# The place of one gate unit, and a parameter tile 40 columns wider

## The chip, the cores and the metric

The kernel runs on one core of a Trainium2 chip. The metric is the time of one execution on the device in microseconds. Five engines work side by side: TensorE (PE; its weight loads are listed apart as PEld), VectorE (DVE), ScalarE (ACT), GpSimd (POOL) and SyncE (SP), which in this kernel issues the transfers (DMA). Every engine runs its own instructions in a fixed order and waits at semaphores for the others.

## What is computed

One layer of a flow-matching backbone over 1152 tokens: 1024 latent ones and 128 of context, each with 1024 channels. Cut to what matters here:

```
proj = h @ w_in                                  # 1024 -> z, xBC, dt, u, v, ga, gb
y_ssd = rmsnorm((scan(conv(xBC), dt) + D*x) * silu(z))
y_sgu = u * (sgu_w @ layernorm(v) + sgu_b)       # in chunks of 128 positions
merged = sigmoid(ga) * (y_ssd @ w_bs) + sigmoid(gb) * (y_sgu @ w_bu)
x = x + gate1 * rmsnorm(merged @ w_out)
up = conv3x3(h2 @ w_up)                          # 1024 -> 2 x 2816
x = x + gate2 * rmsnorm((gelu(up_a) * up_val) @ w_down)
```

All in float32. Each large product is computed with operands split into a high and a low part in a reduced format: high x high, high x low and low x high, so three matmuls per block.

## The kernel before

**Weights.** A class `Weights` (lines 58 to 104) works through one list of weight blocks, `plan`, in which each block is 128 x 512. `_load` brings a block into a raw tile `wr` (three buffers), `_split` makes from it the high part `wh` on ScalarE (L82) and the low part `wl` on VectorE (L83), four buffers each. `advance(n)` splits the next n blocks and keeps loads three ahead; `take(n)` hands out the next n pairs of parts. For some blocks a `room` is given, and their parts go there in place of `wh` and `wl`: six of the eight blocks of each half of v go into `vwh` and `vwl` (lines 891 to 894), and four of the last blocks of the down projection go into `wacc`, which reuses the `acc` tiles (lines 1299 to 1305).

**Units of the input projection.** `inproj` (L422) computes one block of 128 output channels for all tokens: three groups of 24 matmuls over 384 tokens each (`gemm_cm`, L299 to L301), each into a PSUM bank `gps`. Between the groups it splits weights ahead. A `sink` then takes the bank out. There are three such banks (`gbank`), and the v tiles use them too. For a gate unit (`gate_unit`, L615) the sink copies the bank on ScalarE into a tile `gt` (L618) and sends it by a DMA to DRAM (L619), where the merge stage will fetch it. The tile comes from the pool that `gtp.p` names.

**The scan and what comes after.** In the rounds of lines 847 to 869 the scan of 16 head pairs runs beside units of x, z and gates, which fill TensorE. `gtp.p` is then the scan's pool `ssdA`, with one `gt` buffer (L839). Twelve of the 16 gate units run there. The last round is the last z unit alone. L870 closes the scan's pools. The pools opened next lie over the same memory: `right` (with `gt`, now three buffers, L874), `yu` (where `vwh` and `vwl` lie) and `sgu` (with `vtok`). A tile laid over closed ones waits until these are no longer read or written.

Then comes v in two halves (lines 984 to 1004). For each half a gate unit runs first and then nine v tiles (`v_tile`, L901), one per 128 tokens: 24 matmuls with 512 moving columns into one bank, a copy into `vtok` on ScalarE (L910) and statistics on VectorE. Ahead of the first half, `v_ahead(8)` splits all eight blocks of v with a priority 400 places earlier than its place in the program (`P_V`). Two more gate units run behind the eight u units.

**The order.** The instructions of each engine are put in order at compile time: place in the program is the priority, `tc.high_priority(offset=n)` moves a block n places forward, and a model of the engines says when an instruction could start. On the chip, each engine keeps that order.

**The feed-forward part** (from L1164). A pool `ffn` holds the parameters `fpar` (nine taps and a bias for 44 channel blocks), four padded tiles `U`, the accumulators `acc` and the split activations `gh` and `gl`. For each of 22 steps `up_gemm` computes two channel blocks (`pup`), `ffn_conv` applies nine taps (one on ScalarE, eight on VectorE, L1200) and `pair_end` forms gelu times value. `down_mm` (L1207) computes the down projection: 128 tokens of `gh` or `gl` are the weights of a matmul, and 512 columns of `wh` or `wl` are the moving operand, into a bank `fo` (L1212 to L1214). The first third of the tokens is computed in the steps, 18 matmuls at a time, as its activations become ready; the other two thirds follow without a pause, with `gh` and `gl` built from DRAM.

**Places in memory.** The memory of each partition is given out as a stack. The pool `w` has eleven tiles of 2048 bytes (three `wr`, four `wh`, four `wl`). The pools `ssd...`, then `yu`, `sgu` and `br`, and at last `ffn` begin at its end. Inside a pool tiles stand one behind the other, each starting at a multiple of 32 bytes. In `ffn` the order is: `fpar`, four U tiles of 18 x 66 x 4 = 4752 bytes, then `acc`, `gh`, `gl` and the rest.

Of the kernel before, what the change touches and what calls it, by code (L numbers as in the profile page):

```python
# [4 lines left out]
F32 = mybir.dt.float32  # L5
# [25 lines left out]
MT_DT, MT_U, MT_B, MT_C, MT_X, MT_Z, MT_GA, MT_GB = 0, 1, 9, 13, 17, 33, 49, 57  # L31
# [75 lines left out]
def body(tc, A, O):  # L107
# [10 lines left out]
    def close(*cms):  # L118
        for cm in cms:
            cm.__exit__(None, None, None)  # L120
# [10 lines left out]
    ga_scr = dr.tile([8, 128, T], F32, name="ga_scr")  # L131
    gb_scr = dr.tile([8, 128, T], F32, name="gb_scr")
# [17 lines left out]
    gate_mts = [MT_GA + i for i in range(8)] + [MT_GB + i for i in range(8)]  # L150
# [46 lines left out]
    W = Weights(nc, wp, plan)  # L197
# [95 lines left out]
    def gemm_cm(ps, parts, kh, kl, cols, first=True, last=True):  # L293

        n = len(parts) * 4
        for k in range(n):
            wh, wl = (p.rearrange("p (k m) -> p k m", m=128)[:, k % 4, :] for p in parts[k // 4])
            xh, xl = kh[:, k, cols], kl[:, k, cols]
            PE.matmul(ps, lhsT=wh, rhs=xh, start=first and k == 0, stop=False)  # L299
            PE.matmul(ps, lhsT=wh, rhs=xl, start=False, stop=False)  # L300
            PE.matmul(ps, lhsT=wl, rhs=xh, start=False, stop=last and k == n - 1)  # L301
# [11 lines left out]
    def gbank(name):  # L313
        return pg.tile([128, 512], F32, tag="g", name=name)
# [71 lines left out]
    parts = {}  # L386
# [33 lines left out]

    def inproj(sink, parts=None):
        parts = parts or W.take(2)
        for tb in range(NTB):
            ps = gbank("gps")[:, :TB]
            gemm_cm(ps, parts, hh, hl, slice(TB * tb, TB * tb + TB))
            W.advance(1 if tb else 0)
            sink(tb, ps)
            yield  # L430

# [2 lines left out]
    def run_unit(u, step=None):  # L434
        gen, tails = u
        for _ in gen:
            if pending:
                pending.pop(0)()
            if step:
                step()  # L440
        while pending:
            pending.pop(0)()
        pending.extend(tails)
# [119 lines left out]
    def b_unit(g, inp=True):  # L563
        BT = spe.tile([128, GW], F32, tag="BT", name=f"BT{g}")
        Bt = spe.tile([128, NC, 128], F32, tag="Btok", name=f"Btok{g}")
        groups[g] = [BT, Bt]
        return conv_gen(BT, 16 + g, inp), [lambda b=b: to_tok(BT, Bt, f"B{g}", b) for b in range(3)]

    def c_unit(g):
        CT = spb.tile([128, GW], F32, tag="CT", name=f"CT{g}", bufs=2)  # L570

        def cb(b):
            if b == 0:
                groups[g] += [CT, spe.tile([128, 2, NC, 128], F32, tag="CB", name=f"CB{g}")]
            BT, _, _, CB = groups[g]
            pv = tbank(f"pcb{g}{b}")[:, :384].rearrange("p (c i) -> p c i", i=128)
            for i in range(3):
                o = gcol(384 * b + 128 * i)
                PE.matmul(pv[:, i, :], lhsT=BT[:, o:o + 128], rhs=CT[:, o:o + 128], start=True, stop=True)
            for d in range(2):  # L580
                V.tensor_tensor(CB[:, d, 3 * b:3 * b + 3, :], pv, (Lo, Up)[d].unsqueeze(1).to_broadcast([128, 3, 128]), op=ALU.mult)
        return conv_gen(CT, 20 + g), [lambda b=b: cb(b) for b in range(3)]

    def x_unit(q):
        X = spb.tile([128, GW], F32, tag="X", name=f"X{q}", bufs=3)

        def tok(b):
            if b == 0:
                xq[q] = (X, spa.p.tile([128, NC, 128], F32, tag="Xtok", name=f"Xtok{q}", bufs=2))
            to_tok(X, xq[q][1], f"X{q}", b)  # L590
        return conv_gen(X, q), [lambda b=b: tok(b) for b in range(3)]

    def z_unit(q):
        X = xq[q][0]

        def gen():
            zt = spr.tile([128, T], F32, tag="z", name=f"z{q}")

            def sink(tb, ps):
                S.activation(zt[:, TB * tb:TB * tb + TB], ps, AF.Copy, scale=0.5)  # L600
            yield from inproj(sink)
            silu(zt)
            for t0, t1, s in segs(0, T):
                xs = X[:, gcol(t0):gcol(t0) + t1 - t0]
                V.tensor_tensor(xs, xs, zt[:, t0:t1], op=ALU.mult)
                S.activation(zt[:, t0:t1], xs, AF.Square)
            V.tensor_tensor(ssq, ssq, zt, op=ALU.add)
            S.activation(X, X, AF.Copy, scale=par[:, P_SN + q:P_SN + q + 1])
            SP.dma_start(yssd_scr[q], X)
        return gen(), []  # L610
# [1 line left out]
    class gtp:  # L612
        pass

    def gate_unit(dst, parts=None):  # L615
        def sink(tb, ps):
            o = gtp.p.tile([128, TB], F32, tag="gt", name="gt", bufs=gtp.bufs)
            S.copy(o, ps)  # L618
            SP.dma_start(dst[:, TB * tb:TB * tb + TB], o)  # L619
        return inproj(sink, parts), []  # L620

    def unit_of(mt):
        if mt >= MT_GB:
            return gate_unit(gb_scr[mt - MT_GB])
        if mt >= MT_GA:
            return gate_unit(ga_scr[mt - MT_GA])
        if mt >= MT_Z:
            return z_unit(mt - MT_Z)
        if mt >= MT_X:
            return x_unit(mt - MT_X)  # L630
        if mt >= MT_C:
            return c_unit(mt - MT_C)
        return b_unit(mt - MT_B)
# [169 lines left out]
    def merge(fills, steps):  # L803

        nf = 3 * len(fills)
        st = {"k": 0, "d": 0}

        def adv():
            with tc.high_priority(offset=P_SCAN):
                steps[st["d"]]()  # L810
            st["d"] += 1

        def step():
            st["k"] += 1
            while st["d"] < len(steps) * st["k"] // nf:
                adv()
        for f in fills:
            run_unit(unit_of(f), step)
        while st["d"] < len(steps):
            adv()  # L820

    def flush():
        while pending:
            pending.pop(0)()
# [22 lines left out]
    for q in range(17):  # L847
        steps = []
        if q < 16:
            if after is None:  # L850
                flush()
                pro, outs = ssd(q)
                steps += pro + outs
            else:
                steps += after
            after = None
            if q + 1 < 16 and (q + 1) % 4:
                lazy = []

                def nxt_steps(i, q=q, lazy=lazy):  # L860
                    if not lazy:
                        flush()
                        lazy.extend(ssd(q + 1))
                    return lazy[0][i]()
                steps += [lambda i=i, f=nxt_steps: f(i) for i in range(4)]
                after = lazy
        merge(rounds[q], steps)
        if after is not None:
            after = after[1]
    close(sa_cm, sb_cm, se_cm, k_cm, sr_cm)  # L870


# [23 lines left out]
    def v_ahead(n):  # L896

        with tc.high_priority(offset=P_V):
            W.advance(n)
# [74 lines left out]
    def loads(c):  # L974
        if c == 0:
            queue_behind(SP.dma_start(cc.rearrange("p s k -> p (s k)"), A["cond"].to_broadcast([128, 2048])), W.last)
        elif c == 1:
            SP.dma_start(wsT, A["sgu_w"])
            SP.dma_start(sb, A["sgu_b"].to_broadcast([128, 1024]).rearrange("p (g i) -> p g i", g=8))
        elif c < 4:  # L980
            mod_load1()
            mod_load1()

    for h in range(2):
        gate = W.take(2)
        if h == 0:
            v_ahead(8)
        run_unit(gate_unit((gb_scr if gate_mts[h] >= MT_GB else ga_scr)[(gate_mts[h] - MT_GA) % 8], gate))
        if h:
            W.advance(6)  # L990
        parts = W.take(8)
        for c in range(NC):
            cpy = v_tile(h, c, parts)
            if h == 0 and c < 4:
                loads(c)
            if h == 0 and c == 3:
                queue_behind(S.activation(cc, cc, AF.Silu), cpy)
            if h or c >= 4:
                mod_step()
            if h == 0 and c in (6, 7):  # L1000
                bias(c - 6)
            if h and c % 3 == 2:
                layernorm(c // 3)
        W.advance(2)
# [66 lines left out]
    gate = gate_tile(0)  # L1071
# [90 lines left out]


    f_cm, fp = pool("ffn")  # L1164
    fpar = fp.tile([128, 440], F32, name="fpar")
    SP.dma_start(fpar, A["fpar"])

    U = [[fp.tile([128, 18, 66], F32, name=f"U{i}{j}") for j in range(2)] for i in range(2)]
# [66 lines left out]
    for kk in range(NFF):  # L1235
# [19 lines left out]
        else:  # L1255
            for half in range(1 if kk == 1 else 0, 2):
                parts = W.take(2)
# [138 lines left out]
```

## Time and profile before

| | us |
|---|---|
| median of 3 runs | 2447.7 (2444.2 to 2451.8) |
| the profiled execution | 2446.1 |
| its span, first to last instruction | 2444.3 |
| ScalarE busy | 1191.6 |
| DMA, share of 16 engines | 41.1% |

The profile shows one execution. A row of a timeline gives the start from the beginning of the span, the length, the engine, the line, the operation, the tiles written and read, and in brackets the idle time of the engine just before and what ended it. Matmuls overlap: one is shown some 0.33 to 0.40 us long while the next starts 0.17 to 0.23 us behind it, so their spacing is what counts. "128x512" in a matmul's row is the moving operand. A row of a group gives the count, then minimum, median and maximum of the length in ns, or busy time in us and mean length in ns.

### The profile page before, as it was taken

Reading aid. Unit: us, or ns where it says so; the run is one execution under the profiler, and the core shown is the slowest. Engines: PE = TensorE matmul, PEld = TensorE weight load, DVE = VectorE, ACT = ScalarE, POOL = GpSimd, SP = SyncE. Lnnn points to the kernel's source line nnn. Section 1 sums busy time; section 2 is a strip of 40 time slices with the busy share of each in tenths; the row PEclk is TensorE's granted clock in tenths of the full one; section 3 lists DMA queues with packets and bytes.
Section 4 is the critical chain, followed back from the end, with each engine's and each line's share of the span. In section 5 each row is a group of like instructions: output and inputs, shape, how many; then the busy total and the mean of one; then the engine's idle time right before and its main releaser. Section 6 shows DMA issues by size and latency. Waiting matters only on the chain.

```text
span 2444.3 us, 37314 instructions
## 1 busy us (share of the span) xinstructions
PE 2396.7 (98%) x13952; PEld 2267.3 (93%) x13952; DVE 1780.6 (73%) x2754; ACT 1191.6 (49%) x2406; POOL 28.1 (1%) x82
## 2 busy tenths in 40 slices
PE   6989999999999998999999999999999999999998
PEld 4989999999999997899999999999999999998877
DVE  5767787778758764973546657469999989998564
ACT  4586766758647742211435445353333333344443
POOL 0000000000000000000000000000000000000000
PEclk9999999999999999999999999999999999999999
DMA  6144434434424425641556657541222212124674
GB/s 260 35 139 137 120 124 145 136 104 137 140 82 141 152 78 171 214 140 61 162 156 218 198 175 236 155 133 65 69 77 69 72 57 67 61 73 136 216 243 133
DMA packets 204181, 323.20 MB, mean 132 GB/s; under 512 B 19328, under 2 KB 113312, under 8 KB 203872
## 3 DMA queue, kind: packets, MB, share of 16 engines
q1 hardware_dynamic: 204000, 320.82, 41.1%
q8 instruction: 109, 1.79, 0.3%
q14 instruction: 72, 0.59, 0.1%
HBM read 278.22 MB, written 42.52 MB: 131 GB/s over the span
## 4 chain that ended last, share of the span: by engine, by line
PE 90%; DMA 4%; DVE 3%; ACT 1%; issue 1%; SPq 0%; POOL 0%; DVEq 0%; ACTq 0%; POOLq 0%
PE gps L299 11%; PE gps L301 11%; PE gps L300 11%; PE pup L300 7%; PE pup L301 7%; PE pup L299 7%; PE fo L1212 4%; PE fo L1214 4%; PE fo L1213 4%; PE yo L756 2%; PE pbs L301 2%; PE pbs L299 2%; PE pbs L300 2%; PE pv L906 1%; PE pv L907 1%; PE pv L908 1%
## 5 line engine op out<-in xcount | busy, mean ns | idle before, releaser
L83 DVE TENSOR_TENSOR wl<-wr,wh 128x512 fp32r<-128x512 f32 x544 | 372.0, 689 | 270.8 <-ACT wh L82 262.8
L82 ACT CAST wh<-wr 128x512 fp32r<-128x512 f32 x544 | 333.7, 619 | 474.1 <-PE pup L300 121.6
L299 PE MATMUL gps<-hh,wh 128*128 128x384 f32 x1512 | 514.8, 340 | 0.3 <-ACT pad L354 0.3
L301 PE MATMUL gps<-hh,wl 128*128 128x384 f32 x1512 | 513.4, 340 | 0.0
L300 PE MATMUL gps<-hl,wh 128*128 128x384 f32 x1512 | 512.3, 339 | 0.0
L1200 DVE SCALAR_TENSOR_TENSOR acc<-U,fpar,acc 128x960 f32<-128x960 f32 (+1 forms) x352 | 444.2, 1266 | 16.0 <-ACT acc L1193 8.2
L300 PE MATMUL pup<-h2l,wh 128*128 128x384 f32 x1056 | 353.1, 334 | 0.0
L299 PE MATMUL pup<-h2h,wh 128*128 128x384 f32 x1056 | 352.9, 334 | 0.0
L301 PE MATMUL pup<-h2h,wl 128*128 128x384 f32 x1056 | 352.4, 334 | 0.0
L299 PEld LDWEIGHTS gps<-hh,wh 128*128 128x128 f32 x1512 | 284.9, 188 | 2.3 <-issue 1.4
L301 PEld LDWEIGHTS gps<-hh,wl 128*128 128x128 f32 x1512 | 284.7, 188 | 1.7 <-issue 1.7
L300 PEld LDWEIGHTS gps<-hl,wh 128*128 128x128 f32 x1512 | 284.8, 188 | 0.8 <-issue 0.7
L299 PEld LDWEIGHTS pup<-h2h,wh 128*128 128x128 f32 x1056 | 198.2, 188 | 1.4
L300 PEld LDWEIGHTS pup<-h2l,wh 128*128 128x128 f32 x1056 | 198.2, 188 | 1.3
L301 PEld LDWEIGHTS pup<-h2h,wl 128*128 128x128 f32 x1056 | 198.2, 188 | 0.0
L689 ACT ACTIVATE R<-R,nb 128x128 f32<-128x128 f32 x576 | 178.2, 392 | 38.7 <-DMA R<-acs_scr 31.5
L1182 ACT COPY U<-pup 128x384 f32<-128x384 f32 (+1 forms) x132 | 58.4, 442 | 225.2 <-PE pup L301 225.2
L1213 PE MATMUL fo<-wh,gl 128*128 128x512 f32 x384 | 148.3, 396 | 0.0
L1212 PE MATMUL fo<-wh,gh 128*128 128x512 f32 x384 | 148.0, 397 | 0.1
L1214 PE MATMUL fo<-wl,gh 128*128 128x512 f32 x384 | 139.8, 396 | 0.0
L299 PE MATMUL pbs<-ysh,wh 128*128 128x384 f32 x384 | 129.1, 336 | 2.6 <-DVE ga L1110 1.3
L301 PE MATMUL pbs<-ysh,wl 128*128 128x384 f32 x384 | 129.2, 336 | 0.1
(311 smaller groups left out, 3855.5 us busy)
## 6 DMA issues: line engine op xcount, KB each, us to landing
wr<-in_w_dn SPq DMA_DIRECT2D x132, 256.0 KB, 3.0
wr<-in_w_in SPq DMA_DIRECT2D x130, 256.0 KB, 2.8
R<-acs_scr SPq DMA_DIRECT2D x64, 512.0 KB, 4.5
wr<-in_w_bs SPq DMA_DIRECT2D x96, 256.0 KB, 3.4
wr<-in_w_up SPq DMA_DIRECT2D x90, 256.0 KB, 2.6
EP<-acs_scr SPq DMA_DIRECT2D x128, 128.0 KB, 3.2
wmt<-in_w_modt SPq DMA_DIRECT2D x32, 512.0 KB, 3.7
wr<-in_w_bu SPq DMA_DIRECT2D x48, 256.0 KB, 2.9
```

The source lines that it names most:

```text
L82: self.nc.scalar.copy(hi, w)
L83: self.nc.vector.tensor_tensor(lo, w, hi.bitcast(F32), op=ALU.subtract)
L299: PE.matmul(ps, lhsT=wh, rhs=xh, start=first and k == 0, stop=False)
L300: PE.matmul(ps, lhsT=wh, rhs=xl, start=False, stop=False)
L301: PE.matmul(ps, lhsT=wl, rhs=xh, start=False, stop=last and k == n - 1)
L689: S.activation(r, r, AF.Relu, scale=-1.0, bias=nb[:, c, col:col + 1])
L756: PE.matmul(yo[:, d, i, :], lhsT=H[:, k, d, :], rhs=CT[:, 128 * c:128 * c + 128], start=True, stop=True)
L1182: S.copy(u[:, a // 64:b // 64, 1:65], src.rearrange("p (r c) -> p r c", c=64))
L1200: tap = V.scalar_tensor_tensor(av[:, r0:r1], u[:, r0 + dy - 1:r1 + dy - 1, dx:dx + 64], w[i], av[:, r0:r1], op0=ALU.mult, op1=ALU.add)
L1212: PE.matmul(outs[c][h], lhsT=mh[:, cs_], rhs=wh, start=k == 0, stop=False)
L1213: PE.matmul(outs[c][h], lhsT=ml[:, cs_], rhs=wh, start=False, stop=False)
L1214: PE.matmul(outs[c][h], lhsT=mh[:, cs_], rhs=wl, start=False, stop=k == NFF - 1)
```

## The change

Two edits. `inproj` and `gate_unit` lose the argument by which weights were handed in and get a flag `ahead`; without it no weights are split inside the unit. The first gate unit, which ran behind the opening of the new pools, now runs right behind the scan's rounds, ahead of L870, with `ahead` off and with `gt` from the scan's pool. `v_ahead(8)` stays with the first half of v and so stands behind this unit. The second half's gate unit is called as before, by its number. The second edit makes the tile of `fpar` 480 columns wide, of which 440 are used.

```diff
-    def inproj(sink, parts=None):
-        parts = parts or W.take(2)
+    def inproj(sink, ahead=True):
+        parts = W.take(2)
         for tb in range(NTB):
             ps = gbank("gps")[:, :TB]
             gemm_cm(ps, parts, hh, hl, slice(TB * tb, TB * tb + TB))
-            W.advance(1 if tb else 0)
+            if ahead:
+                W.advance(1 if tb else 0)
             sink(tb, ps)
             yield
...
-    def gate_unit(dst, parts=None):
+    def gate_unit(dst, ahead=True):
...
-        return inproj(sink, parts), []
+        return inproj(sink, ahead), []
...
         if after is not None:
             after = after[1]
+
+    run_unit(gate_unit(ga_scr[gate_mts[0] - MT_GA] if gate_mts[0] < MT_GB else gb_scr[gate_mts[0] - MT_GB], False))
     close(sa_cm, sb_cm, se_cm, k_cm, sr_cm)
...
     for h in range(2):
-        gate = W.take(2)
         if h == 0:
             v_ahead(8)
-        run_unit(gate_unit((gb_scr if gate_mts[h] >= MT_GB else ga_scr)[(gate_mts[h] - MT_GA) % 8], gate))
-        if h:
+        else:
+            run_unit(unit_of(gate_mts[h]))
             W.advance(6)
         parts = W.take(8)
...
-    fpar = fp.tile([128, 440], F32, name="fpar")
+
+    fpar = fp.tile([128, 480], F32, name="fpar")[:, :440]
     SP.dma_start(fpar, A["fpar"])
```

## The prediction

> **What bounds the kernel now.** I read the busy shares first, then the chain of work that ended last, then the places where the bounding engine stands still.
>
> ```profile
> PE 2396.7 (98%) x13952; PEld 2267.3 (93%) x13952; DVE 1780.6 (73%) x2754; ACT 1191.6 (49%) x2406; POOL 28.1 (1%) x82
> ...
> PE 90%; DMA 4%; DVE 3%; ACT 1%; issue 1%; SPq 0%; POOL 0%; DVEq 0%; ACTq 0%; POOLq 0%
> ```
>
> TensorE is busy for 98% of the span and carries 90% of the chain. Two things can therefore shorten this kernel: a hole in TensorE's work, or a matmul that takes less time. The change aims at one of each. In the whole trace TensorE's longest idle time after the start-up is at the gate unit ahead of v; here is its timeline there (start, length, line, idle time before and what ended it):
>
> ```profile
> 925.15 0.34 PE L300 MATMUL gps<-hl,wh 128*128 128x384 f32 x1
> 925.33 0.33 PE L301 MATMUL gps<-hh,wl 128*128 128x384 f32 x1
> 925.59 1.09 PE L776 MATMUL yd<-RS,Xtok 128*64 128x128 f32 x16
> 926.51 0.39 PE L776 MATMUL pstc<-RSc,Xtok 128*64 128x128 f32 x4
> 927.32 1.16 PE L756 MATMUL yo<-CT,H 128*128 128x128 f32 x8 [0.42 <-DVE EP L761]
> 936.77 0.79 PE L906 MATMUL pv<-vwh,hh 128*128 128x512 f32 x1 [8.29 <-ACT gt L618]
> ```
>
> The gate's last matmul (L301 at 925.33) is followed by what is left of the scan, and then by 8.29 us of nothing: the first v tile needs one of the three `gps` banks, and all three still hold gate results that ScalarE has not copied out. ScalarE's timeline says why:
>
> ```profile
> 934.00 1.06 ACT L606 ACTIVATE z<-X 128x1024 f32<-128x1024 f32 x1 [2.52 <-DVE X L605]
> 935.09 1.26 ACT L608 ACTIVATE X<-X,par 128x1153 f32<-128x1153 f32 x1
> 936.25 1.22 ACT L618 COPY gt<-gps 128x384 f32<-128x384 f32 x3
> 944.92 0.59 ACT L910 COPY vtok<-pv 128x512 f32<-128x512 f32 x1 [7.44 <-PE pv L908]
> ```
>
> All three copies run in one go at 936.25, behind the last z unit's tail (L606, L608). Their target `gt` lies in the pool opened after the scan, over the scan's RS tiles, which TensorE reads until 926.9. So the copies could not be put into ScalarE's order earlier, although the first of the three matmul groups was over long before. Then the clock, by windows (length, busy times and counts by engine, granted clock, DMA share, GB/s):
>
> ```profile
> 925.00:930.00 5.00, 3.06 (x32) 2.38 (x30) 4.11 (x8) 2.48 (x4) 0.00 (x0) 1.00 0.71 216
> 930.00:935.00 5.00, 0.00 (x0) 0.00 (x0) 3.87 (x8) 1.31 (x2) 0.00 (x0) 0.65 0.31 94
> 935.00:940.00 5.00, 3.23 (x8) 2.56 (x9) 1.36 (x1) 2.44 (x5) 0.00 (x0) 0.50 0.60 140
> 940.00:945.00 5.00, 5.00 (x20) 4.04 (x19) 0.00 (x0) 0.08 (x1) 0.00 (x0) 0.82 1.01 401
> 945.00:950.00 5.00, 5.00 (x24) 4.14 (x23) 0.70 (x1) 0.51 (x1) 0.00 (x0) 1.00 1.01 415
> ```
>
> In the idle time the granted clock falls to 0.50, and it is back only in the course of 940 to 945. The first v tile starts at 936.77 and its copy at 944.92, 8.15 us later. At full clock one tile is 24 x 0.227 = 5.45 us (spacing below), and start to copy about 5.7 us. So the slow restart costs 2.5 us, and the hole as a whole 8.29 + 2.5 = 10.8 us.
>
> **Part one, the gate unit.** No arithmetic changes: the same 72 matmuls, 3 copies and 3 DMAs. The copies now write the scan pool's own `gt`, one buffer, which nothing else overlays. Each can run when its group ends; a group is 24 matmuls at a spacing of about 0.18 us (925.15 to 925.33), so 4.2 us, and the last one ends at 925.66; with scan matmuls between them the three end near 916, 920.5 and 926. Only the buffer's way out can hold them:
>
> ```profile
>   DMA gb_scr<-gt: 1.3, 1
> DMA to landing us min/median/max: 1.8/2.9/5.7
> 936.38 0.33 SPq L609 DMA_DIRECT2D yssd_scr<-X  x1
> yssd_scr<-X SPq DMA_DIRECT2D x2, 576.5 KB, 3.3
> ```
>
> The scan's earlier gate units use this one buffer already, and of all 48 copies one waited for it, 1.3 us. Landing takes 2.9 us, less than a group's 4.2. I take zero; the upper bound is one such 1.3 us, on ScalarE, not on TensorE. The three DMAs move on SP's queue from 937 to 916 to 926, past the loads of E and of the v weights; an issue is 0.33 us and 192 KB compete with loads in a stretch with a DMA share of 0.71. What waits behind them is E (the scan's tail) and the v operands. The latter's last rows in the trace are:
>
> ```profile
> 915.05 1.67 ACT L82 CAST vwh<-wr 128x512 fp32r<-128x512 f32 x3 [3.01 <-PE pstc L741]
> 925.32 0.62 ACT L82 CAST wh<-wr 128x512 fp32r<-128x512 f32 x1 [0.35 <-DMA wr<-in_w_v]
> 925.97 0.69 DVE L83 TENSOR_TENSOR wl<-wr,wh 128x512 fp32r<-128x512 f32 x1 [0.27 <-ACT wh L82]
> ```
>
> The splits start when the scan lets go of Btok (L741, 915.05), which the change does not move, and the eighth is ready at 926.66. A v tile that starts at 928.48 needs it after 7 x 0.68 us, at 933.2: 6.5 us in hand. `v_ahead` now stands behind the gate unit in the program, but its priority of 400 still puts it far ahead.
>
> What is late next? The fourth v tile needs the first one's bank, at 928.5 + 3 x 5.45 = 944.8. That bank's copy writes `vtok`, which lies over the last X; X goes out by a DMA issued at 936.38 that lands in about 3.3 us, 939.7. Five microseconds remain. On ScalarE, the silu of `cc` comes behind the fourth copy, now near 928.5 + 4 x 5.45 = 950.3, when the window to 950 above has just ended with DMA at 1.01; if `cc` were 2 us late, two banks would still cover it. For the second gate unit (h = 1) two splits (0.62 + 0.69 us) move from inside the first gate unit to behind the v tiles; ScalarE is idle there 7.44 us at a time, so I take zero, with 1.3 us as the upper end. TensorE thus goes from yo at 928.48 straight into v: **10.8 us** saved, with 2 us less as the lower end and 0.4 us more (the wait of yo) as the upper.
>
> [...]
>
> **Part two, the wider tile.** The split weights wh and wl are tiles of 2048 bytes per partition, four times 512. The pool `ffn` begins right behind them, so at their offset modulo 512. In it come fpar (440 x 4 = 1760 bytes) and four U tiles (4752 bytes, placed in 4768): 20832 = 40 x 512 + 352. Behind that all tiles that matter (acc 4608, gh and gl 1536) are multiples of 512, so gh and gl stand 352 bytes off wh and wl. With fpar at 1920 bytes the sum is 20992 = 41 x 512, and the offsets are equal. Does that matter? The trace has matmuls of one shape (512 moving columns, 128 weight columns) with both kinds of operands:
>
> ```profile
> L1214 PE MATMUL fo<-wl,gh x384: 390/397/400, 1684.3 to 2436.4; 128*128 128x512 f32 x192
> L1214 PE MATMUL fo<-wacc,gh x12: 387/389/397, 2420.5 to 2433.6; 128*128 128x512 f32 x12
> L908 PE MATMUL pv<-vwl,hh x108: 388/389/628, 937.8 to 1050.1; 128*128 128x512 f32 x108
> L1094 PE MATMUL o<-wl,mh x144: 388/389/398, 1233.2 to 1606.0; 128*128 128x512 f32 x144
> L1093 PE MATMUL o<-wh,ml 128*128 128x512 f32 x144 | 55.4, 392 | 0.0
> L1213 PE MATMUL fo<-wh,gl 128*128 128x512 f32 x384 | 148.3, 396 | 0.0
> ...
> 1010.00:1050.00 40.00, 40.00 (x178) 33.02 (x177) 40.00 (x82) 4.27 (x8) 3.69 (x2) 1.00 0.61 195
> 2250.00:2350.00 100.00, 100.00 (x428) 80.39 (x428) 58.16 (x102) 46.75 (x94) 2.49 (x4) 1.00 0.66 211
> ```
>
> The down projection's usual matmul has a median of 397 ns, and so at unequal offsets. Its last twelve per line take their weights from `wacc`, which lies in acc, in the same pool as gh: equal offsets, 389. The v tiles (389) and the output projection (389) have both operands at one offset too. Ends are modelled, so I check by spacing: a window of length T holds (T + duration)/spacing matmuls. v: 40.39/178 = 227 ns. Down projection: 100.4/428 = 234.6 ns. The difference is 7.5 ns, and TensorE is busy 100% of both windows, so it is TensorE's own time.
>
> How many matmuls gain? There are 3 x 396 = 1188; 36 read wacc and stay equal (acc moves with gh). Of the other 1152, 288 (16 steps of 18) come singly between up projections; these are placed like o, whose mean is 392 with medians of 389, so a part of each step is slow at equal offsets too. They gain 396 - 392 = 4 ns or a little more: 1.2 us. The other 864 run on end and gain 7.5 ns: 6.5 us. Together **7.7 us**. Lower end zero, upper end 1152 x 8 = 9.2 us. In the singles' stretch VectorE is nearly as busy as TensorE:
>
> ```profile
> L1200 DVE SCALAR_TENSOR_TENSOR acc<-U,fpar,acc x352: 1208/1219/1421, 1640.6 to 2238.4; 128x960 f32<-128x960 f32 x132, 128x1152 f32<-128x1152 f32 x44
> 1664.00:1693.00 29.00, 29.00 (x163) 28.19 (x162) 27.57 (x28) 12.49 (x22) 0.00 (x0) 1.00 0.23 75
> ```
>
> 27.57 of 29.00 us; a step that is 0.1 us shorter still fits. The DMA of fpar moves the same bytes into longer rows, at no cost.
>
> [...]
>
> **The sum.** The profiled execution took 2446.1 us, of which 2444.3 is the span; the median of the runs is 2447.7, 1.6 above. 2446.1 - 10.8 - 7.7 = 2427.6; with the 1.6 the forecast is **2429 us**. A measurement of this kernel can tell about 0.3% (7.3 us) from no change.
>
> **The rivals.**
> *TensorE's wait moves.* The gate's copies are early but the v operands are late, since their splits now stand behind the gate in the program. Were the casts to begin only after the last gate copy (926), the eight would need the 11.6 us that they took (915.05 to 926.66) and end at 937.6; the first v tile would end near 938.3 instead of 933.9. That gives back 4.4 us, and up to 2.5 more if the clock falls: 2433 to 2436. If the copies stay behind the z tail after all, part one is worth 0: 2440. Against it: the 6.5 us in hand and the priority. Chance 0.14.
> *Offsets do nothing.* The 8 ns belong to something else in the down projection, say its traffic beside it; part two gives 0 and the time is 2437. Against it: wacc's matmuls run in the same stretch and are fast. Chance 0.08.
> *Neither part works:* 2447. Chance 0.03.
> *Slower: the taps.* The wider tile moves U by 160 bytes and acc with it, and VectorE's taps (16 per step of the up projection, 12 x 1.22 + 4 x 1.42 = 20 us) might dislike the new places. The point from which it decides is the room left: 29.00 - 27.57 = 1.4 us per step, 7% of the taps. At 15% slower taps, 3.0 us a step, 1.6 us over for 22 steps, the stage loses 35 us and with 10.8 + 6.5 gained the time is about 2465. Against it: the four U tiles are 4768 bytes apart, no multiple of 512, so they already stand at four different offsets, and the 960-element taps range only from 1208 ns to a median of 1219. Chance 0.04.
>
> **How the numbers follow.** Both parts as reckoned: 0.71, with 2425 to 2434 for its own range (2 us less from part one, 1.3 from the late splits, the bounds of part two, the spread of the runs). The first rival adds 2433 to 2440 and the second 2437. A range of 2424 to 2438 leaves out the two last rivals, the case of 2440 and a little at the edges, below 2 in 10. Faster by over 0.3% (below 2440.3): 0.71 + 0.14 + 0.08 less 0.05 for edges = 0.88; within 0.3%: 0.08; slower: 0.04.
>
> **What would show it.** Part one is right if the gate's three copies stand apart, each within a microsecond of its matmul group, if no idle time stands before the first pv, and if the granted clock stays 1.00 from 925 to 950. It is wrong if pv waits for vwl, for vtok's copies or for gt. Part two is right if the median of fo falls from 397 to 389 ns and 100 us of the down projection hold 441 or 442 matmuls instead of 428. It is wrong if fo stays at 397, or if TensorE waits for VectorE in the up projection and the taps are above 1219 ns.

## The result, and the profile after

The changed kernel takes 2430.9 us (median of 6 runs, 2426.9 to 2433.5); the kernel before, measured beside it, 2448.9 (6 runs, 2444.2 to 2451.8). The ratio is 0.9928, with a 95% interval of 0.9914 to 0.9941. The forecast was 2429, with a range of 2424 to 2438. The profiled execution took 2430.1 us with a span of 2428.2, 16.1 less than before.

First the page of the changed kernel, busy time by engine and then the shares of the chain that ended last:

```profile
PE 2388.1 (98%) x13952; PEld 2266.0 (93%) x13952; DVE 1781.6 (73%) x2754; ACT 1192.6 (49%) x2406; POOL 27.8 (1%) x82
...
PE 92%; DMA 4%; DVE 2%; ACT 1%; issue 1%; SPq 0%; POOL 0%; DVEq 0%; POOLq 0%; ACTq 0%
```

TensorE still bounds the kernel. Its busy time fell by 8.6 us with the same 13952 matmuls, and its idle time by the other 7.5. These totals alone say little: the two profiles of the kernel before differ by 3.8 us in busy time (2396.7, and 2392.9 in e4 below). What the two edits do shows at the places that the prediction named. TensorE's timeline at the gate unit (lines of the changed file stand one to three higher):

```profile
923.01 0.34 PE L301 MATMUL gps<-hh,wl 128*128 128x384 f32 x1
923.19 0.39 PE L909 MATMUL pv<-vwh,hh 128*128 128x512 f32 x1
...
926.47 1.16 PE L757 MATMUL yo<-CT,H 128*128 128x128 f32 x8 [0.29 <-DVE EP L762]
927.38 0.48 PE L909 MATMUL pv<-vwh,hh 128*128 128x512 f32 x1
```

The first v tile starts 0.18 us behind the gate's last matmul, where 8.29 us of nothing stood before; five of its matmuls even run ahead of the scan's last ones. The windows there (length, busy times and counts by engine, granted clock, DMA share, GB/s) show the clock at 1.00 all along, where it had been 0.65, 0.50 and 0.82:

```profile
925.00:930.00 5.00, 4.71 (x35) 3.78 (x32) 4.17 (x9) 2.49 (x6) 0.00 (x0) 1.00 0.74 248
930.00:935.00 5.00, 5.00 (x24) 4.14 (x23) 3.73 (x6) 1.72 (x3) 0.00 (x0) 1.00 0.19 56
935.00:940.00 5.00, 5.00 (x24) 4.14 (x23) 0.75 (x1) 1.15 (x3) 0.00 (x0) 1.00 0.73 207
940.00:945.00 5.00, 5.00 (x24) 4.14 (x23) 1.98 (x3) 1.16 (x3) 0.00 (x0) 1.00 1.01 388
945.00:950.00 5.00, 5.00 (x24) 4.14 (x23) 0.69 (x1) 1.89 (x3) 0.00 (x0) 1.00 0.88 362
```

ScalarE's timeline has the three gate copies apart, and the v copies behind them:

```profile
912.74 1.66 ACT L82 CAST vwh<-wr 128x512 fp32r<-128x512 f32 x3 [3.01 <-PE pstc L742]
...
914.57 0.48 ACT L619 COPY gt<-gps 128x384 f32<-128x384 f32 x1
...
922.45 0.48 ACT L619 COPY gt<-gps 128x384 f32<-128x384 f32 x1
...
927.96 0.47 ACT L619 COPY gt<-gps 128x384 f32<-128x384 f32 x1
...
934.39 1.26 ACT L609 ACTIVATE X<-X,par 128x1153 f32<-128x1153 f32 x1
939.50 1.07 ACT L913 COPY vtok<-pv 128x512 f32<-128x512 f32 x2 [3.85 <-DMA yssd_scr<-X]
942.64 0.59 ACT L913 COPY vtok<-pv 128x512 f32<-128x512 f32 x1 [2.07 <-PE pv L911]
```

Last the down projection: two groups of matmuls (count, then minimum, median and maximum in ns), the taps (busy us, mean ns), and a window on its run-on part:

```profile
L1216 PE MATMUL fo<-wh,gl x384: 387/389/402, 1665.8 to 2420.0; 128*128 128x512 f32 x192
L1217 PE MATMUL fo<-wl,gh x384: 387/389/397, 1674.4 to 2420.3; 128*128 128x512 f32 x192
```

```profile
L1203 DVE SCALAR_TENSOR_TENSOR acc<-U,fpar,acc 128x960 f32<-128x960 f32 (+1 forms) x352 | 444.2, 1267 | 16.0 <-ACT acc L1196 8.2
```

```profile
2240.00:2340.00 100.00, 100.00 (x442) 82.57 (x442) 60.99 (x108) 47.67 (x95) 3.36 (x5) 1.00 0.71 225
```

The median is 389 ns instead of 397, and 100 us hold 442 matmuls instead of 428.

To see where the time went, the span is cut at matmuls that every kernel has. "Scan" runs from the first `gps` matmul to the last one of the last z unit; "gate" from there to the first matmul of v's second half; "merge" from the first `pbs` to the first `pup`; "fo" from the first to the last `fo` matmul. Every time is a difference of two starts in the traces. The last column is the mean spacing of `fo` matmuls that follow one another, in ns; steps over 0.3 us, which come with waits, are left out. The runs after the first two are explained below.

| kernel | scan | gate | merge | fo | fo spacing |
|---|---|---|---|---|---|
| before | 840.3 | 92.6 | 412.0 | 760.9 | 234.0 |
| changed | 840.0 | 81.8 | 415.1 | 754.7 | 227.4 |
| e1 gate alone | 839.3 | 81.4 | 414.9 | 761.4 | 234.0 |
| e2 tile alone | 840.6 | 92.3 | 414.2 | 754.4 | 227.4 |
| e3 changed, again | 841.3 | 81.4 | 412.4 | 754.8 | 227.4 |
| e4 before, again | 838.8 | 93.2 | 411.5 | 761.6 | 234.0 |
| e5 all shifted | 848.5 | 94.2 | 414.7 | 769.7 | 234.2 |
| e6 offset 256 | 842.0 | 81.6 | 412.1 | 755.1 | 227.4 |
| e7 gl alone | 840.7 | 81.2 | 413.6 | 754.4 | 227.4 |
| e8 own room | 841.9 | 81.3 | 413.5 | 761.4 | 234.0 |
| e9 offset 64 | 839.4 | 81.3 | 411.5 | 761.1 | 233.2 |
| e10 offset 128 | 843.1 | 81.3 | 414.9 | 760.5 | 232.4 |
| e11 four raw tiles | 846.9 | 81.2 | 407.7 | 753.1 | 227.3 |
| e12 four, late | 839.3 | 81.6 | 407.9 | 753.1 | 227.3 |

In the first pair of profiles the 16.1 us are: start-up and scan -2.3, gate -10.8, merge +3.2, feed-forward part -6.2. The gate and the feed-forward part, where the two edits are, come near what was predicted; the two others had not been predicted, and whether the change makes them was open.

### The profile page after: what moved, and what is told of

Its sections match the earlier page's. It is cut to its first block, busy times and chain, and to the rows that moved or that the text cites. A ratio compares the mean times of both kernels' runs of the same rounds, so it can differ in the third digit from the quotient of the medians.

```text
span 2428.2 us, 37315 instructions
## 1 busy us (share of the span) xinstructions
PE 2388.1 (98%) x13952; PEld 2266.0 (93%) x13952; DVE 1781.6 (73%) x2754; ACT 1192.6 (49%) x2406; POOL 27.8 (1%) x82
## 4 chain that ended last, share of the span: by engine, by line
PE 92%; DMA 4%; DVE 2%; ACT 1%; issue 1%; SPq 0%; POOL 0%; DVEq 0%; POOLq 0%; ACTq 0%
PE gps L299 11%; PE gps L301 11%; PE gps L300 11%; PE pup L301 8%; PE pup L300 8%; PE pup L299 8%; PE fo L1215 3%; PE fo L1216 3%; PE fo L1217 3%; PE yo L757 2%; PE pbs L301 2%; PE pbs L299 2%; PE pbs L300 2%; PE pv L911 1%; PE pv L910 1%; PE pv L909 1%
## 5 line engine op out<-in xcount | busy, mean ns | idle before, releaser
L1203 DVE SCALAR_TENSOR_TENSOR acc<-U,fpar,acc 128x960 f32<-128x960 f32 (+1 forms) x352 | 444.2, 1267 | 16.0 <-ACT acc L1196 8.2
```

The lines of the kernel that those rows point to most:

```text
L1203: tap = V.scalar_tensor_tensor(av[:, r0:r1], u[:, r0 + dy - 1:r1 + dy - 1, dx:dx + 64], w[i], av[:, r0:r1], op0=ALU.mult, op1=ALU.add)
```

## The experiments

**Each half alone, and both kernels again.** e1 is the changed kernel with the narrow tile, e2 the kernel before with the wide one; e3 and e4 repeat the two kernels on the same chip.

```diff
 # e1, on the changed kernel
-    fpar = fp.tile([128, 480], F32, name="fpar")[:, :440]
+    fpar = fp.tile([128, 440], F32, name="fpar")
 # e2, on the kernel before
-    fpar = fp.tile([128, 440], F32, name="fpar")
+    fpar = fp.tile([128, 480], F32, name="fpar")[:, :440]
```

> Only the gate unit is moved; fpar stays 440 columns wide. Theory (the hole closes, nothing else): the hole before the first v tile, 8.29 us idle and 2.5 us of slow clock, is gone and the time falls by 10.8 us, to 0.9956 of before; the median length of fo stays at 397 ns. In the changed kernel's profile the merge stage (from the first pbs to the first pup) took 415.1 us instead of 412.0 before. Rival (the edit costs the merge stage something, since the merge stage's gt tiles now lie elsewhere in the right pool): 3.2 us of the gain are given back there, the time falls by only 7.6 us, and TensorE again waits for wh near the second block of tokens. Rival (those 3.2 us are chance): the merge stage is at 412 to 413 us here, or anywhere between 412 and 415 in every kernel.

> Only fpar's tile is 480 columns wide; the gate unit stays behind the opening of the new pools. Theory (equal offsets make the down projection's matmuls shorter): fo's median falls from 397 to 389 ns, and from the first fo to the last 6 to 8 us go; the hole of 8.29 us before v stays; the time falls by 6 to 8 us, to 0.997 of before. Rival (the offsets do nothing by themselves, and fo became faster through something in the gate edit): fo stays at 397 and the ratio is 1.000. Rival (VectorE's taps suffer from the new places): taps above 1219 ns and no gain in the up projection.

> The changed kernel once more, for a second profile. If the 3.2 us lost in the merge stage and the 0.8 us of idle time in the last third of the down projection (near 2350) belong to the change, they stand in this profile again; if they are chance, the merge stage takes 412 us and the down projection has one wait of under 0.1 us. Time 0.9928 of before either way, within 0.0015.

> The kernel before once more, for a second profile. The hole before v is 8.3 us again with a slow clock behind it, and fo is at 397 ns: both follow from the order and the places. The start (to the first gps at 69.6) and the merge stage (412.0) may differ by some microseconds if these are the parts that vary from one execution to the next.

Against 2446.94 us for the kernel before: e1 2433.97, ratio 0.9945 (0.9933 to 0.9958); e2 2440.62, ratio 0.9971 (0.9959 to 0.9982); e3 2427.54, ratio 0.992 (0.9905 to 0.9935); e4, one run, 2443.31. The halves are worth 13.0 and 6.3 us, 19.3 together, and e3 is 19.4 below: they add up. The table says where: e1 changes "gate" alone and e2 "fo" alone. It also bears on the two differences that nobody predicted. The same program has 415.1 and 412.4 us in "merge" (changed, e3). The -2.3 is for the most part the start: the first `gps` matmul stands at 69.6 us in the first profile before and at 67.6 in the changed kernel, but at 67.4 in e4. So nothing here puts the -2.3 or the +3.2 of the first pair down to the change; both lie within what one kernel varies by, or close to it.

One part of the difference in "merge" can be read from the traces. Near 1498 TensorE waits for a cast of `wh`. First the changed kernel, then e3, each with the row of this wait and the window behind it:

```profile
1498.84 0.44 PE L299 MATMUL pbs<-ysh,wh 128*128 128x384 f32 x1 [1.56 <-ACT wh L82]
1500.00:1505.00 5.00, 5.00 (x19) 4.61 (x18) 4.62 (x11) 2.86 (x6) 0.00 (x0) 0.67 0.77 257
```

```profile
1498.03 0.44 PE L299 MATMUL pbs<-ysh,wh 128*128 128x384 f32 x1 [1.24 <-ACT wh L82]
1500.00:1505.00 5.00, 5.00 (x27) 4.59 (x26) 4.61 (x11) 3.10 (x5) 0.00 (x0) 1.00 0.93 327
```

In the changed kernel the clock is 0.50 in each half microsecond from 1500.0 to 1503.0, 0.70 in the next and 1.00 from 1503.5 to 1505.0. Its 0.67 over the whole window is 3.3 us at half clock, an estimated cost of 1.7 us: 19 matmuls start where e3 has 27. Seven traces have such a slow stretch in "merge" (changed, e1, e2, e5, e6, e8, e10), and their mean there is 414.2 us; the five others with three raw tiles have 412.2. The wait alone does not decide it: e7 waits 1.52 us at this place and keeps a clock of 1.00.

**Is it the gate unit's place, or the room of `gt`?** e8 is the kernel before with the gate unit where it was, behind the new pools, but with `gt` in a pool of its own that lies over no scan tile.

```diff
+    gx_cm, gxp = pool("gtx", side=RT)
...
-    gtp.p, gtp.bufs = rp, 3
+    gtp.p, gtp.bufs = gxp, 3
```

> The kernel before, the gate unit still behind the opening of the new pools and behind v_ahead, with weights split inside it as before, but gt lies in a small pool of its own that overlays nothing (three buffers, opened ahead of the scan and kept). fpar is 440 columns wide. Theory (the copies were late only because gt's room was not free): the three copies stand apart, each behind its matmul group, the hole before v is gone, and the time from the end of the last z unit to the second half of v is 81.5 us as in the changed kernel instead of 92.7; 11 us less than before, ratio 0.9955. Rival (the gate unit had to stand ahead of v's splits in the program, or had to stop splitting weights itself): a wait of several microseconds before v remains, for vwl or for the banks, and the ratio is 0.998 to 1.000.

Measured 2436.45 us against 2444.87, ratio 0.9958 (0.9941 to 0.9974), 8.4 us less; the gate stage is 81.3 us, as in the changed kernel, 11.4 below the mean of the kernels with the hole. ScalarE's and TensorE's rows in e8:

```profile
917.76 0.48 ACT L619 COPY gt<-gps 128x384 f32<-128x384 f32 x1
...
923.49 0.47 ACT L619 COPY gt<-gps 128x384 f32<-128x384 f32 x1
...
929.22 0.47 ACT L619 COPY gt<-gps 128x384 f32<-128x384 f32 x1
```

```profile
926.20 0.34 PE L301 MATMUL gps<-hh,wl 128*128 128x384 f32 x1
926.38 0.39 PE L907 MATMUL pv<-vwh,hh 128*128 128x512 f32 x1
```

The copies stand apart and v follows the gate after 0.18 us, though the unit's place in the program is the old one and weights are still split inside it. So the room of the target is the cause, and moving the unit was one way to give it room. (e8 also takes the merge stage's `gt` tiles from the new pool.)

**Does the offset matter, or the down projection?** e5 puts 160 bytes ahead of the weight pool in the kernel before, and leaves the order of work on every engine as it was. All weight tiles and everything behind them move by 160 bytes; `hh`, `hl` and the feed-forward input do not. So v, the input units and the up projection, whose operands stood at one offset, now have unequal ones, the down projection keeps its 352, and the merge stage's `pbs` matmuls, whose operands both move, keep equal ones.

```diff
+    pw_cm, pw = pool("padw")
+    pw.tile([128, 40], F32, name="padw")
```

> The kernel before (fpar 440 columns, gate unit where it was) with 160 unused bytes per partition ahead of the weight pool. wh, wl and everything allocated behind them move by 160 bytes: gh, gl and wacc come to 32 modulo 512, where they lie in the changed kernel, but wh and wl go from 32 to 192, so the two stay 352 apart; hh and hl stay at 32, so the v tiles' operands, equal before, are now 160 apart. The order of instructions is that of before on every engine. Theory (what counts is that both operands of a matmul have the same offset): fo stays at 397 ns, with wacc's too now at about 397 no more than before (389, equal pair), v's matmuls rise from 389 to about 393 to 397 ns, and the time is up to 3 us longer than before. Rival (what counts is the place of gh and gl alone, 32 modulo 512): fo falls to 389 ns and v stays at 389. For the matmuls with 384 columns no row says what unequal offsets cost; they are over 10000, so at 1 ns each the time rises by 10 us.

One run: 2469.33 us against 2444.87, 24.5 us slower. Rows of e5:

```profile
L910 PE MATMUL pv<-vwl,hh x108: 392/397/628, 944.4 to 1058.9; 128*128 128x512 f32 x108
```

```profile
L302 PE MATMUL gps<-hl,wh x1512: 331/338/522, 67.3 to 1203.5; 128*128 128x384 f32 x189
```

```profile
L302 PE MATMUL pup<-h2l,wh x1056: 336/338/423, 1619.7 to 2245.1; 128*128 128x384 f32 x176
```

And the same two groups of 384 columns in the kernel before:

```profile
L300 PE MATMUL gps<-hl,wh x1512: 331/334/522, 69.8 to 1193.0; 128*128 128x384 f32 x189
```

```profile
L300 PE MATMUL pup<-h2l,wh x1056: 334/334/418, 1606.4 to 2221.6; 128*128 128x384 f32 x176
```

v goes from 389 to 397 ns, and in mean spacing from 227.1 to 234.3, nearly the pair of values that the down projection has with and without the wide tile. Could the new place alone be the cause, whatever the other operand does? The matmuls whose operands both moved by 160 bytes say no: `pbs` stays at a median of 334 ns, and in e5 those on `wacc` have their 389 of before:

```profile
L1214 PE MATMUL fo<-wacc,gh x12: 388/389/397, 2443.2 to 2456.3; 128*128 128x512 f32 x12
```

The 384-column matmuls lose too, 334 to 338 ns, in mean spacing 178.1 to 180.8 (`gps`) and 173.6 to 176.8 (`pup`). By count: 4536 x 2.7 + 3168 x 3.2 + 432 x 7.2 ns = 12.2 + 10.1 + 3.1 = 25.4 us, and 24.5 were measured. What the 384-column matmuls would lose had been left open (10 us at 1 ns each); by this count it is nine tenths of the price.

**Which offsets are equal?** The text before the result speaks of offsets modulo 512. Three more widths of the parameter tile, and one change to `gl` alone, test the number. In the changed kernel:

```diff
-    fpar = fp.tile([128, 480], F32, name="fpar")[:, :440]
+    fpar = fp.tile([128, 544], F32, name="fpar")[:, :440]   # e6: gh, gl 256 bytes off
+    fpar = fp.tile([128, 496], F32, name="fpar")[:, :440]   # e9: 64 bytes off
+    fpar = fp.tile([128, 512], F32, name="fpar")[:, :440]   # e10: 128 bytes off
...
-        ml = fp.tile([128, TB], F32R, tag="gl", name=f"gl{nm}{k}", bufs=bufs)
+        ml = fp.tile([128, TB + 128], F32R, tag="gl", name=f"gl{nm}{k}", bufs=bufs)[:, 64:64 + TB]   # e7
```

> The changed kernel with fpar's tile 544 columns wide instead of 480: gh and gl then lie 256 bytes (half of 512) off wh and wl, where before they lay 352 off. The order of instructions is that of the changed kernel. Theory (any unequal offset costs): fo's spacing is 230 to 236 ns instead of 227, and the stretch from the first fo to the last is 2 to 8 us longer than in the changed kernel (754.7 us). Rival (512 has nothing to do with it; 256 or less is the period): fo stays at 227 ns as if the offsets were equal. Rival (the cost grows with the distance from a multiple of 512): spacing above the 234 of before, since 256 is the farthest possible.

> The changed kernel, but gl alone is moved: its tiles are 128 columns wider and the values stand 64 columns (256 bytes) in, so that gl lies 256 off, and gh, wh, wl and wacc stay equal. Only every third matmul (L1216, which loads gl as its weights) has unequal operands. Theory (a matmul's stream and the weight load of the next one, which runs beside it, disturb each other): a third of the loss of the run with all at 256 appears, and the starts show it in one of the three matmuls: the step from L1215 to L1216 is longer, the others stay at 227 ns. Rival (the pairing shifts the whole rhythm): all three steps are longer.

> The changed kernel with fpar's tile 496 columns wide: gh, gl and wacc lie 64 bytes off wh and wl. So far 352 and 160 gave a spacing of 234 ns, and 0 and 256 gave 227. All four fit a period of 64, of 128 or of 256 bytes; a period of 32 is out, since 352 is a multiple of it. Period 64: spacing 227 ns, the stretch from the first fo to the last 754.7 to 755.1 us as in the changed kernel. Period 128 or 256: spacing 230 ns or more, and the stretch 757 to 761 us.

> The changed kernel with fpar's tile 512 columns wide: 128 bytes off. Period 64 or 128: spacing 227 ns and the stretch from the first fo to the last 754.7 to 755.1 us. Period 256: spacing 230 ns or more and 757 to 761 us. With the run at 64 this leaves one period.

One run each: e6 2428.81 and e7 2428.37 us beside 2444.87 for the kernel before; e9 2436.19 and e10 2438.12 beside 2447.03. The same group of matmuls in e6, e9 and e10, in this order:

```profile
L1216 PE MATMUL fo<-wh,gl x384: 389/389/398, 1664.2 to 2418.8; 128*128 128x512 f32 x192
```

```profile
L1216 PE MATMUL fo<-wh,gl x384: 391/394/398, 1665.6 to 2426.2; 128*128 128x512 f32 x192
```

```profile
L1216 PE MATMUL fo<-wh,gl x384: 387/393/405, 1668.2 to 2428.1; 128*128 128x512 f32 x192
```

At 256 bytes off nothing is lost: 389 ns and a spacing of 227.4, the same as at 0. The theory that e6 started from, 230 ns or more, was wrong, and its first rival came true. At 64 and 128 bytes it is 394 and 393 ns (233.2 and 232.4), at 352 and, in e5, at 160 it is 397 (234.0, and 234.3 in v). So of the six differences measured, 0 and 256 bytes cost nothing, and 64, 128, 160 and 352 cost 5.0 to 7.2 ns a matmul; what other differences cost was not measured. e7, which put 256 bytes between `gl` and the others and was meant to show whether one of three matmuls alone loses, lost nothing, like e6: 389 in all three. What one unequal operand of three costs was not measured at an offset that costs anything.

**A fourth raw weight tile.** Some of TensorE's idle time that is left in the changed kernel is at casts that wait for weights. The waits of TensorE in "merge" (in all, times, longest, in us), for the changed kernel and then for e3:

```profile
PE pbs L299 <- ACT wh L82: 3.6, 3, 1.6
PE pht L284 <- DVE mm L1151: 0.4, 1, 0.4
PE pht L284 <- ACT hf L287: 0.4, 1, 0.4
PE pbu L299 <- ACT wh L82: 0.2, 1, 0.2
```

```profile
PE pbs L299 <- ACT wh L82: 1.2, 1, 1.2
PE pbs L299 <- DVE ga L1112: 1.1, 1, 1.1
```

e11 is the changed kernel with four `wr` buffers and loads four ahead, everywhere. e12 has the fourth tile (`wx`, in the pool `right`, for every fourth block) and the four loads ahead only behind v.

```diff
 # e11
-    def __init__(self, nc, pool, plan, ahead_load=3):
+    def __init__(self, nc, pool, plan, ahead_load=4):
...
-        w = self.pool.tile([128, 512], F32, tag="wr", name=f"wr{self.nl}", bufs=3)
+        w = self.pool.tile([128, 512], F32, tag="wr", name=f"wr{self.nl}", bufs=4)
 # e12
+        if self.more and (self.nl - self.more[1]) % 4 == 3:
+            w = self.more[0].tile([128, 512], F32, tag="wx", name=f"wx{self.nl}", bufs=1)
+        else:
+            w = self.pool.tile([128, 512], F32, tag="wr", name=f"wr{self.nl}", bufs=3)
...
+    W.al, W.more = 4, (rp, W.nl)
```

> The changed kernel with four raw weight tiles wr in place of three and loads four ahead in place of three (2048 bytes more, so all offsets modulo 512 stay). This changes the order of instructions in many places, from the start on. In the changed kernel TensorE still waits for weights: some 3 to 4 us in the merge stage and 0.8 us near 2350. Theory (these waits are late loads): they shrink, and the time falls by 1 to 4 us below that of the changed kernel, ratio to before about 0.991. Rival (they come from the order on ScalarE, not from loads, or the new order opens others): no gain, or a loss of some microseconds; ratio 0.992 to 0.996.

> The changed kernel with a fourth raw weight tile (every fourth block, in a pool of its own on the right side) and loads four blocks ahead, switched on only behind the two halves of v, so that the order of work up to the u units stays that of the changed kernel. If the merge stage's waits are TensorE waiting for raw weight tiles and the longer scan of the kernel with four raw tiles everywhere came from its new order: scan 840 to 843 us, merge stage (first pbs to first pup) 412 to 415 falls to about 408, first to last fo matmul 754.7 falls to about 753, the time about 6 us below the changed kernel's, some 2422 us, ratio to the kernel before about 0.9895. Rival, that the waits only move (ScalarE casts in another order, or the loads crowd other transfers): merge stage at 411 or more and the time within 2 us of the changed kernel's 2428 to 2431.

e11: 2426.98 us against 2447.03, ratio 0.9915 (0.9899 to 0.9932). Merge falls to 407.7 and fo to 753.1, but the scan grows to 846.9 and eats most of it. New waits of TensorE up to the gate, rows of e11 that the changed kernel does not have:

```profile
PE yo L757 <- DVE H L733: 2.8, 1, 2.8
...
PE yd L777 <- DVE X L784: 0.9, 1, 0.9
PE pst L727 <- DVE xwf L712: 0.8, 1, 0.8
```

The order on TensorE differs from that of the changed kernel from the 118th matmul on, and in the scan, where VectorE feeds TensorE, it is worse by 4.5 us of such waits. That the new order makes these waits was not tested apart from the loads.

e12: **2419.85 us** against 2447.23, ratio 0.9889 (0.9873 to 0.9906), below the changed kernel's first interval (from 0.9914) and at the edge of its second (from 0.9905). The numbers come out as expected or a little better: scan 839.3, merge 407.9, fo 753.1. Against the mean of the changed kernel, e3, e6 and e7 (413.3 and 754.7) that is 5.4 + 1.6 = 7.0 us. Its waits in "merge":

```profile
PE pbs L303 <- ACT wh L86: 0.6, 1, 0.6
PE o L1101 <- DVE wl L87: 0.3, 1, 0.3
```

Against the first profile of the changed kernel the waits listed shrink by 3.7 us (4.6 to 0.9) and the stage by 7.3. The slow stretch near 1500, which e12 does not have, is some 1.7 us more. A `pbs` matmul is shown 334 ns long (median) at a spacing of some 180, so a delay shorter than the difference does not appear as idle time, which may be the rest, but that was not tested. The tile and the deeper loads come together in e12; which of them does it was not separated.

## Why the prediction was right

**Part one, 10.8 us: measured 11.2.** The mean gate stage of before, e4 and e2 is 92.7 us; that of the changed kernel, e1, e3, e6 and e7 is 81.5. In the first pair it is 10.8. The cause, three copies held by the room of `gt`, is shown by e8. The restart at half clock went with the hole: the granted clock is 1.00 in every window from 925 to 950.

Three steps inside it were less good than the sum. The test "each copy within a microsecond of its group" was missed: the groups' last matmuls end at 913.23, 918.29 and 923.35, the copies follow 1.3, 4.2 and 4.6 us later. The first stands behind three casts (912.74), the third behind another cast (927.45). The second is held longer because the buffer's way out is longer than the 2.9 us of landing that the prediction reckoned with. The DMA of the first copy, done at 915.05, is issued on SP's queue only at 919.23, behind loads and stores, and lands at 922.35; the second copy starts at 922.45 (SP's rows):

```profile
916.93 1.06 SPq L745 DMA_DIRECT2D out<-so  x2
918.85 0.34 SPq L70 DMA_DIRECT2D wr<-in_w_v  x1
919.23 0.63 SPq L620 DMA_DIRECT2D gb_scr<-gt  x1
...
935.68 0.33 SPq L610 DMA_DIRECT2D yssd_scr<-X  x1
```

The time in the queue that a transfer is moved into was taken as nothing; it was 4.2 us. It cost TensorE nothing: the second v tile, which takes the second bank, starts at 931.56 (row below), and the copy ends at 922.93. The "what is late next" step found the right wait: the first v copy waits for X to go out and runs at 939.50, forecast 939.7. But the room behind it is 2.4 us, not 5, and in e1 it is 1.0: that copy ends near 940.0 and the fourth v tile starts at 942.44. The whole stage lies 2.3 us earlier in this profile, while X's DMA moved up by only 0.7 (936.38 to 935.68). And the last split of the v operands ends 5.5 us ahead of the matmul that reads it, where 6.5 were reckoned; VectorE's row of it and TensorE's rows:

```profile
925.12 0.69 DVE L83 TENSOR_TENSOR wl<-wr,wh 128x512 fp32r<-128x512 f32 x1 [1.90 <-ACT wh L82]
```

```profile
931.34 0.39 PE L911 MATMUL pv<-wl,hh 128*128 128x512 f32 x1
931.56 0.39 PE L909 MATMUL pv<-vwh,hh 128*128 128x512 f32 x1
```

As for the slow restart in the kernel before, a clock of 0.82 from 940 to 945 is 1.8 us at half, so it was back at 941.8 (by half microseconds it is 0.50 up to 941.5, 0.72 in the next and 1.00 from 942.0), 5.0 us after 936.77. The 2.5 us in the sum are half of these 5.0. The rival "TensorE's wait moves" did not come true.

**Part two, 7.7 us: measured 6.7.** The fo stretch is 761.3 us on average over the four kernels at 352 bytes (before, e1, e4, e8) and 754.7 over the five at 0 or 256. Of it, 0.9 us is in the 288 matmuls between the up projections, where 1.2 was predicted, and 5.8 us in those that run on end, where 6.5 was. The 7.5 ns each were not what was off: e5 at unequal offsets and e12 at equal ones have no wait in the run-on part, and there it takes 210.4 and 203.8 us, 6.7 us less over 864 matmuls, or 7.7 ns each. What the sum put at nothing is waiting. The five at 0 or 256 all wait for a cast of `wh` near 2350, e3 by 0.9 us in all; the kernel before has no such wait, e1, e4 and e8 one of 0.5. The changed kernel's row (in all, times, longest, in us):

```profile
PE fo L1215 <- ACT wh L82: 0.6, 1, 0.6
```

Steps over 0.3 us in the run-on part take 1.46 us more than the spacing in these five on average, and 0.75 in the four at 352 bytes; the difference is the 0.7 us that is missing. With four raw tiles there is no such step, which is nearly all of the 1.6 us that e11 and e12 gain in "fo". The taps are as long as before (1267 ns mean, before 1266), so the rival on VectorE fell, and "offsets do nothing" fell with e2 and e5.

One step was right for the wrong number. The prediction takes 512 bytes as the modulus, by which 256 bytes off would be unequal; e6 loses nothing there (a spacing of 227.4 ns). The forecast needed only 352 and 0, which the runs show at 234.0 and 227.4 ns, so it did not notice; that was luck.

The sum was 18.5; the two stages give 11.2 + 6.7 = 17.9, and the medians differ by 18.0 in the first comparison and by 19.4 in e3.

## What to carry to other kernels

When a producer's result waits for a copy, look at where the copy's target lies: in the kernel before it lay over tiles that were read until 926.9, the three copies ran only at 936.25, and TensorE stood for 8.29 us with all three banks full; room of its own for that target took 11 us off the stage. Where matmuls of one shape and this format show two lengths in one trace (397 and 389 ns here), compare the places of moving and weight operands early: differences of 0 and 256 bytes cost nothing in these runs, 64, 128, 160 and 352 cost 5.0 to 7.2 ns. Look also at the waits for weights behind matmuls that became faster: here the longer steps of the run-on part took 1.46 us beyond the spacing instead of 0.75. Deeper prefetch is worth trying stage by stage: switched on everywhere (e11) it lost in the scan (846.9 us) most of what it won in the stages behind; switched on behind v, with one more tile (e12), it won 7 us.

## What the hardware showed that was not expected

- The place of the operands cost 512-column matmuls 5.0 to 7.2 ns of 227 at differences of 64, 128, 160 and 352 bytes (e9, e10, e5 and the kernel before) and nothing at 0 and 256 (the changed kernel, e6); 384-column ones lost 2.7 and 3.2 ns of 178.1 and 173.6 at 160 bytes (e5), the only difference tried for them.
- The half clock came behind a short hole too: in the changed kernel for some 3.3 us behind a wait of 1.56 us (clock 0.67 from 1500 to 1505), while e7 kept 1.00 behind one of 1.52 us.
- The same program differed by 2.7 us in one stage between two runs (merge, 415.1 and 412.4), as much as many an edit is worth; a difference between two single profiles needs a second pair before it is explained.
